# Sums over a head's features as products with a column of ones, in a one-core hybrid decoder layer

## The chip, the cores and the metric

The program runs on one core of a Trainium2 chip. The metric is the time of one execution on the device in microseconds (us); the runs of the kernel before have a median of 665.29 us.

## What is computed

One decoder layer over 256 tokens of width 1024, in float32. A normed input goes through one combined projection (`w_in`) that feeds four token mixers: A, attention; B, a chunked gated DeltaNet; C, an RWKV-7 recurrence; D, a Mamba-2 SSD. Each mixer's output goes through its own projection, is gated and summed, goes through `w_out` and is added to the input; then comes a SwiGLU feed-forward part. The change touches three sums over the 64 features of a head: RWKV's squared length of `kk` and its `bonus`, and DeltaNet's squared lengths of q and k.

```python
def l2norm(x):
    xf = x.astype(jnp.float32)
    return xf * lax.rsqrt(jnp.sum(xf * xf, axis=-1, keepdims=True) + 1e-6)
...
        o_b = gated_deltanet(l2norm(heads(g_q)) * (Dh ** -0.5), l2norm(heads(g_k)),
                             heads(g_v), beta, g_log)
...
        kk = l2norm(heads(c_k * rwkv_k_k[i]))
...
        bonus = jnp.sum(r_h * k_h * rwkv_r_k[i], axis=-1, keepdims=True) * v_h
```

## The kernel before

Every large product has a float32 weight matrix that is split in two parts, `whi` and `wlo` (rounded to a one-pass format), and a split activation. Weights come in pieces of 128x1024: SyncE loads `wraw`, ScalarE casts it to `whi`, VectorE subtracts to get `wlo`, and each piece then feeds 24 products of 256 columns on TensorE, 8 of them with `wlo`. These "large products" (`pj`, `pjt`, `pbr`, `pjo`, `pjf`; `pd` in the last stage) fill TensorE from the first to the last microsecond.

The mixers run between them. Features lie on partitions, two heads of 64 to a tile; a tile of one tensor is [128, 4, 256] (two heads by 64 features, four pairs, 256 tokens). A head's part of 64 tokens is a 64x64 block, and work on it uses 64x64 tiles of the array, two at a time. `stacked` turns such blocks over by a product with the identity, so that tokens lie on partitions: 16 calls for half of a tensor, into a PSUM tile `ptk`. Each call of a float32 product is two instructions in the trace (and two weight loads). The block is the stationary operand, the identity the moving one.

RWKV (`rwkv_mix`): `kkr` and `rkr` (tile `a`) are turned over in halves, ScalarE squares the turned `kkr` into `U`, and VectorE sums over features with TENSOR_REDUCE into `rk2` (shown as `rk`) and `bon`. Then eight groups of `pab` products make the matrix `U` that is inverted (`inverse`: a trip through DRAM as `Du`, `UL`, a loop on VectorE over `TL`, a trip as `Dz`, `TN`, and products `pq`, `pt`, `pq`, `pn`). Four chunk steps follow (`pA`, `pB`, `pH`, `pY`), then a tail of VectorE work (group norm, bonus) up to the products `py`; "c" is done behind it. DeltaNet (`gdn_mix`) has the same shape: `tokens(0)` turns `KQ[:, 0]` over, squares it (`sq`), sums it (`sse`) and keeps the turned block as `Kt`; `tokens(1)` does so for q later on, for the sum alone.

The order on each engine is not written out: a planner (class `Queue`, `Chain`, `run`) simulates the engines while the program is recorded, with a cost for each instruction in `Queue.cost`, and chooses from the ready steps of the mixers' chains and the large products. Each engine then runs its instructions in that recorded order. All are recorded in one helper, so all rows have line L180. PSUM has two banks in the pool `pa` for the mixers and two in `px`.

Of the kernel before, what the change touches and what calls it, by code (L numbers as in the profile page):

```python
# [10 lines left out]
AF = mybir.ActivationFunctionType  # L11
OP = mybir.AluOpType
AX = mybir.AxisListType
# [154 lines left out]
class Queue:  # L168
# [98 lines left out]
    def cost(self, op, a, k, n, ins, start):  # L267
        if self.idx == 0:
            w = a[1]
            t = int(start / 3.413)  # L270
            if t != self.tick:
                self.warm = t == self.tick + 1 and self.cols >= 3060
                self.tick, self.cols = t, 0.0
            one = op == "transpose" or w.dtype != F32
            self.cols += n * (1 if one else 2) * w.shape[0] / 128
            tiling = tuple(32 if x <= 32 else 64 if x <= 64 else 128 for x in (w.shape[0], math.prod(w.shape[1:])))
            if op == "transpose":
                d = 0.109 * n / 128
            elif one:
                d = 0.006 + 0.00043 * n  # L280
            elif tiling[0] == 32:
                d = 0.018
            elif tiling == (64, 64):
                d = 0.058 if n <= 64 else 0.003 + n / 1200
            else:
                d = max(0.22, 0.006 + n / 600)
            if tiling != self.tiling:

                d += 0.2 if tiling == (128, 128) else 0.14
                self.tiling = tiling  # L290
            return d * (1 if self.warm else 1.95)
        if self.idx == 1:
            if op == "tensor_tensor" or op == "tensor_sub" or op == "tensor_reduce":
                return 0.065 + 0.00105 * n if op != "tensor_reduce" else 0.07 + 0.00105 * math.prod(ins[0].shape[1:])
            if op == "scalar_tensor_tensor":
                return 0.12 + 0.00105 * n
            return 0.065 + (0.0064 if op == "reciprocal" else 0.0009) * n
        if self.idx == 2:
            d = 0.047 + 0.00088 * n + (0.1 if hasattr(k.get("scale"), "shape") or hasattr(k.get("bias"), "shape") else 0.0)
            s = _SETS.get(a[2] if len(a) > 2 else None)  # L300
            if s is not None and s != self.table:
                self.table = s
                d += 1.3
            return d
        if k.get("op") == OP.pow:
            return 0.3 + 0.165 * n
        return 0.1 + {"tensor_tensor": 0.0019, "tensor_sub": 0.00215, "tensor_copy": 0.0016}.get(op, 0.001) * n
# [3 lines left out]
def trunk(ctx: ExitStack, tc: tile.TileContext, I, out):  # L311
    nc = tc.nc
    clock = Clock(tc)
    T, V, A, G, SY = [Queue(clock, i, e) for i, e in enumerate((nc.tensor, nc.vector, nc.scalar, nc.gpsimd, nc.sync))]
# [213 lines left out]
    ones = cst.tile([128, 1], F32, name="ones")  # L528
# [61 lines left out]
    def p_(n, j=None, k=1):  # L590
        o, w = PO[n]
        if j is None:
            return PR[:, o:o + w]
        return PR[:, o + j:o + j + k]
# [35 lines left out]
    def du_rows(h):  # L630

        return bass.AP(tensor=Du.tensor, offset=Du.offset + 4160 * h, ap=[[64, 64], [8320, 16], [1, 64]])
# [8 lines left out]
    def ui(c, pp=0):  # L641

        return (c % 2) * 8 + (c // 2) * 4 + pp

    def t2(name, shape=(128, 4, 256)):
        return wk.tile(list(shape), F32, name=name, tag="t2", bufs=T2)
# [16 lines left out]
    def bank(name):  # L663
        return pa.tile([128, 512], F32, name=name, tag="pa")
# [13 lines left out]
    def halves(fn):  # L678
        for h in range(2):
            fn(h, slice(h * 64, (h + 1) * 64))  # L680
# [8 lines left out]
    def trh(out, x):  # L689

        for s in (slice(0, 64), slice(64, 128)):
            T.matmul(out[s], x[s], ident[s, s], start=True, stop=True)

    def inverse(U, N64):

        halves(lambda h, s: SY.dma_start(du_rows(h), U[s]))
        for k in range(4):
            s, o = 32 * k, 32 * (k % 2)
            G.tensor_copy(uo[s:s + 16, :, 16:32], U[s:s + 16, :, o + 16:o + 32])
        TL = wk.tile([128, 16, 16], F32, name="TL", tag="TL", bufs=1)  # L700
# [50 lines left out]
        for u in range(16):  # L751
            for h in range(2):
                T.matmul(pq[blk[2 * h + 1], u], U[blk[2 * h], u, 32:64], T16[blk[2 * h], u], start=True, stop=True)
        for h in range(2):
# [9 lines left out]
    def stacked(src, half):  # L764

        pt = bank("ptk").rearrange("p (u e) -> p u e", u=8)
        for c in (half, half + 2):
            for pp in range(4):
                trh(pt[:, ui(c, pp) - 8 * half], src[:, pp, c * 64:(c + 1) * 64])
        return pt, slice(8 * half, 8 * half + 8)  # L770

    def stacked_copy(src, dst):
        for half in range(2):
            pt, us = stacked(src, half)
            A.copy(dst[:, us], pt)
# [186 lines left out]
    def rwkv_mix():  # L962
        ck, cr, cvv = rst[0], rst[1], rst[2]
        W, Wi, a = rws["W"], rws["Wi"], rws["a"]
        kkr, ka = t2("kkr"), t2("kka")
# [25 lines left out]
        Bb, Kb, rkr = ka, Wi, kr  # L991
# [3 lines left out]
        for q in two:  # L995
            V.tensor_tensor(Kb[:, q], kr[:, q], Wi[:, q], op=OP.mult)
            yield
        for pp in range(4):
            V.scalar_tensor_tensor(rkr[:, pp], cr[:, pp], p_("rk", pp), kr[:, pp], op0=OP.mult, op1=OP.mult)
            if pp % 2:  # L1000
                yield 1
        U = t2("U", (128, 16, 64))
        rk2, bon = [wk.tile([128, 16], F32, name=n, tag=n, bufs=1) for n in ("rk2", "bon")]
        for half in range(2):
            pt, us = stacked(kkr, half)
            A.activation(U[:, us], pt, AF.Square)
            pt, us = stacked(rkr, half)
            V.tensor_reduce(bon[:, us], pt, op=OP.add, axis=AX.X)
            V.tensor_reduce(rk2[:, us], U[:, us], op=OP.add, axis=AX.X)
            yield 0  # L1010
        V.tensor_scalar(rk2, rk2, 2.0, 2e-6, op0=OP.mult, op1=OP.add)
        V.reciprocal(rk2, rk2)
        yield 0

# [1 line left out]
        for c in (0, 2, 1, 3):  # L1016
            for q in two:
# [5 lines left out]
                us = slice(ui(c, q.start), ui(c, q.stop))  # L1023
# [6 lines left out]
        wait = next(inv)  # L1030
        Vst, Bt, Kt = [t.rearrange("p q (a b) -> p (q a) b", b=64) for t in (cr, cvv, ck)]
        stacked_copy(cvv, Vst)
        yield 0
        stacked_copy(Bb, Bt)
        yield 0
        stacked_copy(Kb, Kt)
        yield wait
        yield from inv
# [4 lines left out]
        for c in range(4):  # L1043
            us = slice(ui(c), ui(c) + 4)
            cs = slice(c * 64, (c + 1) * 64)
            pA = cbank("pA")
            for pp in range(4):
                u = ui(c, pp)
# [12 lines left out]
            if c < 3:  # L1061
                pH = cbank("pH")
                for pp in range(4):
                    u = ui(c, pp)
# [10 lines left out]
            for pp in range(4):  # L1075
                u = ui(c, pp)
# [99 lines left out]
    def gdn_mix():  # L1176
# [3 lines left out]
        KQ, Vt, zs = gst_["kq"], gst_[2], gst_[3]  # L1180
        sq = t2("sq", (128, 16, 64))
        sse = wk.tile([128, 2, 16], F32, name="sse", tag="sse", bufs=1)
        store = a3("gst3", (128, 3, 16, 64))
        Kt, At, Vn = store[:, 0], store[:, 1], store[:, 2]
        DL = DLs[0]

        def tokens(kq):

            for half in range(2):
                pt, us = stacked(KQ[:, kq], half)  # L1190
                A.activation(sq[:, us], pt, AF.Square)
                if kq == 0:
                    A.copy(Kt[:, us], pt)
                yield 0
                V.tensor_reduce(sse[:, kq, us], sq[:, us], op=OP.add, axis=AX.X)
            V.tensor_scalar(sse[:, kq], sse[:, kq], 4e-6, None, op0=OP.add)

        yield KQ
        yield from tokens(0)
        yield  # L1200
        nk = wk.tile([128, 16], F32, name="nk", tag="nk", bufs=1)
        V.tensor_scalar(nk, sse[:, 0], 0.25, None, op0=OP.mult)
# [10 lines left out]
        U = t2("gU", (128, 16, 64))  # L1213
        for c2 in range(2):
            for a in range(2):
                pab = bank("pab").rearrange("p (u e) -> p u e", u=4)
                us = slice(ui(2 * a + c2), ui(2 * a + c2) + 4)
# [10 lines left out]
        for half in range(2):  # L1228
            pvn, us = stacked(Vt, half)
            V.tensor_tensor(Vn[:, us], pvn, nk[:, us, None].to_broadcast([128, 8, 64]), op=OP.mult)  # L1230
        yield 0
        yield from tokens(1)
        yield wait
        yield from inv
        yield N64
# [2 lines left out]
        for c in range(4):  # L1238
            us = slice(ui(c), ui(c) + 4)
# [538 lines left out]
    for k in "AC":  # L1778
        ytile(k)
    Chain("mix", when(has("common"), then("g", rwkv_gates())), when(lambda: len(ready_c) == 6, then("c", rwkv_mix())),  # L1780
          when(lambda: len(ready_b) == 8 and "dec" in done, then("b", gdn_mix())))
    Chain("fill", when(has("common"), scalars()), when(has("g"), attn_bias()), *[then(f"a{g}", attn[g][1]()) for g in range(2)], then("dec", decays()),
          *[then(f"d{g}", when(has("A"), mam[g][1]())) for g in range(2)])
# [14 lines left out]
    sq = cst.tile([128, 2, 4], F32, name="sq2")  # L1798
# [188 lines left out]
```

## Time and profile before

| | |
|---|---|
| median of 3 runs | 665.29 us (663.74 to 665.30) |
| profiled execution, time | 665.81 us |
| its span | 663.9 us |
| busy: PE, VectorE, ScalarE, GpSimd | 643.4, 442.9, 306.3, 44.6 us |
| mean granted TensorE clock | 0.991 |
| longest group on VectorE | `wlo`, 176 of 1.22 us: 213.8 us |
| longest group on ScalarE | `whi`, 176 of 1.05 us: 183.1 us |

PE's busy time counts modelled ends of pipelined products, so it is an upper bound. What counts is where PE waits, and what the clock was. The feed-forward part (from 475 us) and the input part (to 138 us) are the same work in the same order in both kernels.

### The profile page before, as it was taken

To read this page: it belongs to the slowest core of one execution; us is meant where nothing else is said; L and a number is where in the kernel's file an instruction comes from. 1 tells how busy PE (TensorE), PEld (TensorE's weight loads), DVE (VectorE), ACT (ScalarE), POOL (GpSimd) and SP (SyncE) were. 2 spreads that over 40 slices of the span, in tenths; PEclk is the share of its full clock that TensorE was granted. 3 is DMA by queue.
4 is the path that set the end of the run, shared out by engine and by line. 5 is a ranking of instruction groups with operands and counts; after the bars stand their busy time and mean duration, and the time that the engine had idled before them with its cause. 6 is when DMAs were issued, how large, how long until landed. Compare 5 with 4: busy or idle time off the path is not lost.

```text
span 663.9 us, 15583 instructions
## 1 busy us (share of the span) xinstructions
PE 643.4 (97%) x6677; PEld 605.7 (91%) x6677; DVE 442.9 (67%) x769; ACT 306.3 (46%) x484; POOL 44.6 (7%) x48
## 2 busy tenths in 40 slices
PE   8999999899998988999999999999999999999997
PEld 7799999899897878999999989999999999998885
DVE  4575567966864389888678367777676666664443
ACT  5465465433534254465433343444554544454331
POOL 1001003003400020100210002000000000000000
PEclk9999999989999988999999999999999999999999
DMA  8534845324182123255466433665565555555551
GB/s 287 159 128 154 281 147 160 120 65 129 41 244 69 35 64 128 96 193 160 156 168 177 136 97 97 220 223 165 158 199 189 183 189 191 190 182 181 189 178 64
DMA packets 47866, 102.80 MB, mean 155 GB/s; under 512 B 19980, under 2 KB 24501, under 8 KB 47798
## 3 DMA queue, kind: packets, MB, share of 16 engines
q1 hardware_dynamic: 47562, 101.25, 48.1%
q8 instruction: 52, 0.85, 0.5%
q10 hardware_dynamic: 236, 0.58, 0.2%
q14 instruction: 16, 0.13, 0.1%
HBM read 99.17 MB, written 4.21 MB: 156 GB/s over the span
## 4 chain that ended last, share of the span: by engine, by line
PE 85%; DVE 6%; ACT 3%; DMA 2%; issue 1%; POOL 0%; DVEq 0%; SPq 0%; ACTq 0%; POOLq 0%
PE pj L180 25%; PE pjf L180 19%; PE pd L180 9%; PE pjt L180 6%; PE pbr L180 5%; PE pjo L180 4%; PE ptk L180 2%; DVE wlo L180 2%; PE pab L180 2%; DMA TN<-Dz 1%; PE pA L180 1%; PE psx L180 1%; PE po L180 1%; PE pY L180 1%; PE pB L180 1%
## 5 line engine op out<-in xcount | busy, mean ns | idle before, releaser
L180 DVE TENSOR_TENSOR wlo<-wraw,whi 128x1024 fp32r<-128x1024 f32 x176 | 213.8, 1221 | 68.5 <-ACT whi L180 67.5
L180 ACT CAST whi<-wraw 128x1024 fp32r<-128x1024 f32 x176 | 183.1, 1049 | 143.0 <-PE pj L180 39.0
L180 PE MATMUL pj<-HT,whi 128*128 128x256 f32 x1120 | 154.3, 286 | 0.4 <-ACT HT L180 0.2
L180 PEld LDWEIGHTS pj<-HT,whi 128*128 128x128 f32 x1120 | 139.9, 189 | 5.1 <-issue 3.0
L180 PE MATMUL pjf<-HT,whi 128*128 128x256 f32 x704 | 91.2, 281 | 0.0
L180 PEld LDWEIGHTS pjf<-HT,whi 128*128 128x128 f32 x704 | 86.7, 188 | 0.1
L180 PE MATMUL pj<-HT,wlo 128*128 128x256 f32 x560 | 80.5, 284 | 0.8 <-DVE wlo L180 0.8
L180 PEld LDWEIGHTS pj<-HT,wlo 128*128 128x128 f32 x560 | 71.6, 188 | 1.6 <-DVE wlo L180 1.2
L180 PE MATMUL pd<-whi,gt 128*128 128x512 f32 x176 | 54.8, 393 | 0.0
L180 PE MATMUL pjf<-HT,wlo 128*128 128x256 f32 x352 | 49.2, 281 | 0.0
L180 PEld LDWEIGHTS pjf<-HT,wlo 128*128 128x128 f32 x352 | 44.9, 188 | 0.0
L180 PEld LDWEIGHTS pd<-whi,gt 128*128 128x128 f32 x176 | 33.0, 188 | 7.4
L180 PE MATMUL pjt<-whi,HT 128*128 128x256 f32 x256 | 37.9, 302 | 0.9 <-ACT whi L180 0.9
L180 PEld LDWEIGHTS pjt<-whi,HT 128*128 128x128 f32 x256 | 35.0, 207 | 2.2 <-ACT whi L180 1.3
L180 PE MATMUL pd<-wlo,gt 128*128 128x512 f32 x88 | 34.5, 393 | 0.0
L180 DVE TENSOR_TENSOR gu<-pjf,rB 128x512 f32<-128x512 f32 x22 | 15.2, 691 | 17.4 <-PE pjf L180 17.3
L180 PE MATMUL pjt<-wlo,HT 128*128 128x256 f32 x128 | 19.1, 286 | 2.5 <-DVE wlo L180 2.5
L180 PEld LDWEIGHTS pd<-wlo,gt 128*128 128x128 f32 x88 | 16.5, 188 | 3.8
L180 PEld LDWEIGHTS pjt<-wlo,HT 128*128 128x128 f32 x128 | 16.7, 191 | 3.0 <-DVE wlo L180 3.0
L180 ACT CAST gt<-sg 128x256 fp32r<-128x256 f32 x22 | 8.9, 406 | 20.9 <-DVE sg L180 20.9
L180 PE MATMUL pjo<-whi,ms 128*128 128x256 f32 x128 | 17.8, 284 | 0.0
L180 DVE TENSOR_TENSOR gt<-sg,gt 128x256 fp32r<-128x256 f32 x22 | 9.4, 425 | 11.8 <-ACT gt L180 11.8
(395 smaller groups left out, 836.0 us busy)
## 6 DMA issues: line engine op xcount, KB each, us to landing
wraw<-in_w_in_dram SPq DMA_DIRECT2D x86, 512.0 KB, 4.3
wraw<-in_ffn_in_dram SPq DMA_DIRECT2D x44, 512.0 KB, 3.7
wraw<-in_ffn_down_dram SPq DMA_DIRECT2D x22, 512.0 KB, 3.7
wraw<-in_w_branch_dram SPq DMA_DIRECT2D x16, 512.0 KB, 5.1
wraw<-in_w_out_dram SPq DMA_DIRECT2D x8, 512.0 KB, 4.4
D<-Dv SPq DMA_DIRECT2D x1, 1536.0 KB
E<-D SPq DMA_DIRECT2D x8, 128.0 KB, 3.4
xm<-in_x_dram SPq DMA_DIRECT2D x4, 256.0 KB, 5.2
```

The lines of the kernel that those rows point to most:

```text
L180: bi = fn(*a, **k)
```

## The change

A new function `sums` makes the sum over features with the block as the stationary operand and a column of ones as the moving one: 32 calls of one column for each tensor, into a PSUM tile `pss`. In RWKV the four `stacked` and four TENSOR_REDUCE go; ScalarE squares all of `kkr` in one instruction from SBUF (into `U`), `sums` takes `U` and `rkr`, and VectorE reads the sums from PSUM, with one more small copy for `bon`. In DeltaNet `tokens` goes; both squares and both sums come at the start, and `stacked_copy` makes `Kt` where `tokens(1)` stood. One number of the planner's cost table changes: a 64x64 call with n of at most 64 columns was 0.058 us and is 0.03 + 0.00044 n.

```diff
             elif tiling == (64, 64):
-                d = 0.058 if n <= 64 else 0.003 + n / 1200
+                d = 0.03 + 0.00044 * n if n <= 64 else 0.003 + n / 1200
...
+    def sums(*src):
+
+        ps = bank("pss")[:, :16 * len(src)].rearrange("p (k u) -> p k u", u=16)
+        for k, x in enumerate(src):
+            for c in range(4):
+                for pp in range(4):
+                    for s in (slice(0, 64), slice(64, 128)):
+                        T.matmul(ps[s, k, ui(c, pp):ui(c, pp) + 1], x[s, pp, c * 64:(c + 1) * 64], ones[s], start=True, stop=True)
+        return ps
...
+        U = t2("U", (128, 16, 64))
+        A.activation(U.rearrange("p (q a) b -> p q (a b)", q=4), kkr, AF.Square)
...
-        for half in range(2):
-            pt, us = stacked(kkr, half)
-            A.activation(U[:, us], pt, AF.Square)
-            pt, us = stacked(rkr, half)
-            V.tensor_reduce(bon[:, us], pt, op=OP.add, axis=AX.X)
-            V.tensor_reduce(rk2[:, us], U[:, us], op=OP.add, axis=AX.X)
-            yield 0
-        V.tensor_scalar(rk2, rk2, 2.0, 2e-6, op0=OP.mult, op1=OP.add)
+        ps = sums(U.rearrange("p (q a) b -> p q (a b)", q=4), rkr)
+        V.tensor_scalar(rk2, ps[:, 0], 2.0, 2e-6, op0=OP.mult, op1=OP.add)
+        V.tensor_copy(bon, ps[:, 1])
...
-        yield KQ
-        yield from tokens(0)
+
+        sqv = sq.rearrange("p (q a) b -> p q (a b)", q=4)
+        for kq in range(2):
+            yield KQ
+            A.activation(sqv, KQ[:, kq], AF.Square)
+            yield 1
+            V.tensor_scalar(sse[:, kq], sums(sqv)[:, 0], 4e-6, None, op0=OP.add)
...
-        yield from tokens(1)
+        stacked_copy(KQ[:, 0], Kt)
```

Since the planner's picture of time changes, the order of all that follows changes on every engine. Three places:

TensorE, where RWKV's sums are made (`ptk` and `pss` as above, `pab` the first group behind them; x counts calls). Before:

```order
L180 MATMUL pjt<-wlo,HT_78 128x256 x4
L180 MATMUL ptk<-ident,kkr 64x64 x16
L180 MATMUL ptk<-ident,a 64x64 x16
L180 MATMUL pjt<-wlo,HT_78 128x256 x4
L180 MATMUL pj<-HT_78,whi 128x256 x8
L180 MATMUL ptk<-ident,kkr 64x64 x16
L180 MATMUL ptk<-ident,a 64x64 x16
L180 MATMUL pab<-AR,kka 64x128 x2
```

TensorE at the same place, now:

```order
L180 MATMUL pjt<-wlo,HT_78 128x256 x4
L180 MATMUL pss<-ones,U 64x1 x32
L180 MATMUL pss<-ones,a 64x1 x32
L180 MATMUL pab<-AR,kka 64x128 x2
L180 MATMUL pab<-AR,Wi 64x128 x2
```

The twelve large products that stood between the turned blocks now come later.

ScalarE in RWKV's inverse (`kkr<-TN` and `TN<-pq` are the inverse's copies; `pn` on TensorE needs the latter). Before:

```order
L180 CAST whi<-wraw 128x1024 x2
L180 COPY kkr<-TN 32x16x32 x4
L180 CAST whi<-wraw 128x1024 x2
L180 COPY TN<-pq 32x512 x2
L180 ACTIVATE gate<-pj 128x512
```

ScalarE in RWKV's inverse, now:

```order
L180 CAST whi<-wraw 128x1024
L180 COPY kkr<-TN 32x16x32 x4
L180 COPY TN<-pq 32x512 x2
L180 ACTIVATE gate<-pj 128x512
L180 CAST whi<-wraw 128x1024
```

The two casts between the two kinds of copies have moved to behind them.

VectorE, the last rows of RWKV's tail (`kka` is RWKV's output, `bc` and `cvt` a convolution of mixer D, `xd`, `zt` also D's; `U<-py` ends the tail). Before:

```order
L180 SCALAR_TENSOR_TENSOR bc<-pj,PR,bc 128x255
L180 TENSOR_TENSOR kka<-kka,kc 128x512
L180 TENSOR_TENSOR wlo<-wraw,whi 128x1024
L180 TENSOR_TENSOR kka<-kka,grsd 128x512
L180 TENSOR_TENSOR kka<-kka,PR 128x512
L180 SCALAR_TENSOR_TENSOR bc<-pj,PR,bc 128x254
L180 TENSOR_TENSOR kka<-kka,kc 128x512
L180 SCALAR_TENSOR_TENSOR bc<-pj,PR,bc 128x253
L180 TENSOR_TENSOR wlo<-wraw,whi 128x1024 x2
L180 SCALAR_TENSOR_TENSOR bc<-pj,bc 128x256
L180 SCALAR_TENSOR_TENSOR zt<-zt,pjt 128x512
L180 SCALAR_TENSOR_TENSOR U<-py,PR,U 128x256 x4
```

VectorE, the last rows of the same tail, now:

```order
L180 TENSOR_TENSOR zt<-dx,zt 128x256
L180 SCALAR_TENSOR_TENSOR cvt<-pj,PR,cvt 128x253
L180 SCALAR_TENSOR_TENSOR bc<-pj,PR,bc 128x254
L180 TENSOR_TENSOR kka<-kka,kc 128x512
L180 TENSOR_SCALAR ms<-ms 128x1
L180 SCALAR_TENSOR_TENSOR cvt<-pj,cvt 128x256
L180 SCALAR_TENSOR_TENSOR bc<-pj,PR,bc 128x253
L180 TENSOR_TENSOR wlo<-wraw,whi 128x1024
L180 TENSOR_SCALAR zt<-zt,ms 128x256
L180 SCALAR_TENSOR_TENSOR bc<-pj,bc 128x256
L180 SCALAR_TENSOR_TENSOR U<-py,PR,U 128x256 x4
```

From the first operation behind the last `P<-pB` to `U<-py`, the tail held six `wlo` and eight `bc` operations before and holds four and four now; the rest of these have moved to behind `U<-py`.

## Rows read from the trace of the kernel before

**Rows 1.** The page, part 1 and the granted clock of part 2 (40 slices of the span, tenths).
```profile
PE 643.4 (97%) x6677; PEld 605.7 (91%) x6677; DVE 442.9 (67%) x769; ACT 306.3 (46%) x484; POOL 44.6 (7%) x48
...
PEclk9999999989999988999999999999999999999999
```

**Rows 2.** Busy time by stretch: us, PE, PEld, DVE, ACT, POOL, PEclk, DMA share, GB/s.
```profile
138.60:194.20 55.60, 54.96 (x724) 49.92 (x723) 40.24 (x82) 26.22 (x44) 13.56 (x16) 1.00 0.37 99
194.20:231.10 36.90, 34.79 (x885) 31.52 (x885) 14.90 (x28) 11.36 (x22) 1.75 (x3) 1.00 0.25 84
231.10:259.60 28.50, 23.62 (x207) 22.12 (x206) 25.50 (x51) 13.46 (x27) 3.46 (x2) 0.88 0.23 74
```

**Rows 3.** Timeline of PE: start, us, then the instructions (two for each float32 call).
```profile
138.61 1.15 PE L180 MATMUL ptk<-ident,kkr 64*64 64x64 f32 x32
...
144.20 0.44 PE L180 MATMUL pab<-AR,kka 64*64 64x128 f32 x4
...
159.31 2.08 PE L180 MATMUL ptk<-ident,kka 64*64 64x64 f32 x64
161.23 2.03 PE L180 MATMUL ptk<-ident,Wi 64*64 64x64 f32 x64
```

**Rows 4.** Single tiles: count, ns min/median/max, first and last start, array tile and shape.
```profile
L180 PEld LDWEIGHTS ptk<-ident,kkr x64: 129/135/135, 138.6 to 143.1; 64*64 64x64 f32 x64
...
L180 PEld LDWEIGHTS pst<-sc,ident x16: 132/138/138, 48.3 to 48.7; 128*64 128x64 f32 x16
...
L180 PEld LDWEIGHTS pe<-dA,C x8: 189/192/192, 166.1 to 166.9; 128*128 128x128 f32 x8
...
L180 DVE TENSOR_REDUCE sse<-sq x4: 680/686/686, 319.2 to 339.8; 128x8 f32<-128x512 f32 x4
...
L180 ACT CAST whi<-wraw x176: 1034/1049/1058, 10.6 to 651.4; 128x1024 fp32r<-128x1024 f32 x176
```

**Rows 5.** The chain that ended last, in order of time: start, us, what.
```profile
187.77 6.38 DMA TN<-Dz
194.19 1.24 PE pq L180 x79
...
251.95 5.08 PE pjt L180 x28
...
267.14 0.86 PE pyd L180 x8
...
283.83 33.61 PE pj L180 x284
```

**Rows 6.** Timeline of ACT in RWKV's inverse, and of PE behind it.
```profile
202.95 2.50 ACT L180 COPY kkr<-TN 32x512 f32<-32x512 f32 x4 [9.85 <-DVE TN L180]
205.48 1.99 ACT L180 CAST whi<-wraw 128x1024 fp32r<-128x1024 f32 x2
207.50 1.18 ACT L180 COPY TN<-pq 32x512 f32<-32x512 f32 x2
...
208.73 1.19 PE L180 MATMUL pn<-TN 32*32 32x32 f32 x62 [0.36 <-ACT TN L180]
```

**Rows 7.** Timeline of RWKV's tail: its ends on DVE, and PE's longest wait.
```profile
231.78 0.42 DVE L180 TENSOR_TENSOR P<-pB,rk 128x256 f32<-128x256 f32 x1 [2.54 <-PE pB L180]
...
251.95 0.91 PE L180 MATMUL pjt<-wlo,HT 128*128 128x256 f32 x4 [1.62 <-DVE wlo L180]
...
261.05 1.65 DVE L180 SCALAR_TENSOR_TENSOR U<-py,PR,U 128x256 f32<-128x256 f32 x4
```

**Rows 8.** Groups of DVE instructions: count, busy us, mean ns, idle before.
```profile
L180 DVE TENSOR_TENSOR wlo<-wraw,whi 128x1024 fp32r<-128x1024 f32 x176 | 213.8, 1221 | 68.5 <-ACT whi L180 67.5 <-issue 0.7
...
L180 DVE SCALAR_TENSOR_TENSOR bc<-pj,PR,bc 128x254 f32<-128x254 f32 x4 | 1.9, 470 | 0.0
```

**Rows 9.** Busy time by stretch around the first fall of the clock (columns as in rows 2).
```profile
129.00:132.40 3.40, 1.75 (x11) 1.41 (x10) 3.40 (x10) 1.09 (x3) 0.00 (x0) 1.00 0.45 154
132.40:135.80 3.40, 3.39 (x18) 3.39 (x18) 3.40 (x7) 0.00 (x0) 0.00 (x0) 0.57 0.51 163
```

**Rows 10.** Timeline: DeltaNet's output, from its last products to its first use.
```profile
417.49 2.08 PE L180 MATMUL py<-ident,O 64*64 64x64 f32 x64
...
421.42 1.28 DVE L180 TENSOR_TENSOR yB<-gvz,yB 128x512 fp32r<-128x512 f32 x2
...
436.18 1.12 PE L180 MATMUL pbr<-yB,whi 128*128 128x256 f32 x8
```

More of the change, by code (lines that the diff above doesn't have):

```diff
@@ L1001, in rwkv_mix @@
                 yield 1
-        U = t2("U", (128, 16, 64))
         rk2, bon = [wk.tile([128, 16], F32, name=n, tag=n, bufs=1) for n in ("rk2", "bon")]
-        for half in range(2):
-            pt, us = stacked(kkr, half)
-            A.activation(U[:, us], pt, AF.Square)
-            pt, us = stacked(rkr, half)
-            V.tensor_reduce(bon[:, us], pt, op=OP.add, axis=AX.X)
-            V.tensor_reduce(rk2[:, us], U[:, us], op=OP.add, axis=AX.X)
-            yield 0
-        V.tensor_scalar(rk2, rk2, 2.0, 2e-6, op0=OP.mult, op1=OP.add)
+        ps = sums(U.rearrange("p (q a) b -> p q (a b)", q=4), rkr)
+        V.tensor_scalar(rk2, ps[:, 0], 2.0, 2e-6, op0=OP.mult, op1=OP.add)
+        V.tensor_copy(bon, ps[:, 1])
         V.reciprocal(rk2, rk2)
@@ L1185, in gdn_mix @@
         DL = DLs[0]
[L1187 to L1196, printed above, removed]
-        yield KQ
-        yield from tokens(0)
+        sqv = sq.rearrange("p (q a) b -> p q (a b)", q=4)
[4 more added lines that the diff above has]
+            V.tensor_scalar(sse[:, kq], sums(sqv)[:, 0], 4e-6, None, op0=OP.add)
         yield
```

## The prediction

> **What bounds the kernel now.** I read the page first: PE is busy for 97% of the span, VectorE for 67%, and the granted clock dips in three slices of 40 [rows 1]. So the time is PE's own work plus the places where PE waits or runs at the lower clock, and an engine that is relieved counts only where PE waits for it. Next I cut the span into stretches. From RWKV's sums to the first `pq`, PE is busy for 54.96 of 55.60 us; through the inverse and the four chunk steps for 34.79 of 36.90 us; through RWKV's tail for 23.62 of 28.50 us, at a mean clock of 0.88 [rows 2]. At full clock the tail holds 23.62 x 0.88 = 20.8 us of PE work, so 7.7 us are lost there, the largest loss of the kernel. VectorE is the reason: the tail lasts from the last `P<-pB` to `U<-py`, 231.78 to 261.05 us, 29.3 us, and PE's longest wait in it, 1.62 us, is for a `wlo` [rows 7]. The other two losses are on a chain: `pq` starts at 194.19, when the DMA `TN<-Dz` lands, with no gap between them [rows 5], and `pn` waits for ScalarE's copy `TN<-pq`, which stands behind two casts of 1.99 us [rows 6]. The eight reductions that the change removes are not in any of these places. What the change does to the time is therefore PE's own sum, and what the new order does at these three places.
>
> **PE's own work.** A turned block costs, from the starts of two neighbouring runs of 32 calls, (161.23 - 159.31) / 32 = 0.060 us per call [rows 3]. RWKV's four `stacked` (64 calls) and DeltaNet's four in `tokens` (64) go: 128 x 0.060 = 7.7 us. `stacked_copy` for `Kt` brings 32 back: +1.9 us. The 128 calls of one column are new. No row shows a 64x64 tile with one column, so I bound it. Above: the same tile with 64 columns, 0.060. Below: the 32x32 tile, where 64 calls of `pq` take 1.24 us [rows 5], 0.019 each. The nearest row is `pst`, 64 columns of weights and 8 moving: 16 instructions start between 48.3 and 48.7 us [rows 4], 0.4/15 = 27 ns each, 0.053 for a call of two. And its weight load takes 138 ns, that of a turned block 135, that of a 128-column block 192: the load goes by the columns of the weights, and the change leaves those at 64. So I take 0.057, close to the upper end: 128 x 0.057 = 7.3 us. PE's work changes by -7.7 + 1.9 + 7.3 = **+1.5 us**, with ends of -3.4 (at 0.019) and +1.9 (at 0.060).
>
> The Trainium skill speaks against this part of the change. "TensorEngine Tiling (Array Packing)", Instruction Overhead, says that a matmul with one column takes as long as one with 60; by it the sums would cost what the turned blocks cost and the work would be +1.9. The row of `pst` agrees so far as it goes (8 columns, hardly cheaper than 64).
>
> **What leaves the other engines.** Eight reductions of 0.68 us [rows 4] leave VectorE and one small copy comes: about -5 us, but at 140 to 145 and 319 to 340 us, where PE does not wait for VectorE. Cover: PE has large products queued there, so this is worth nothing by itself. ScalarE squares a whole tensor at once, about 1.05 us (its cast of the same 1024 elements, [rows 4]). In DeltaNet this square now stands ahead of PE's `pss`, with large products queued in front; without them PE would wait up to 1.05 us, twice. DVE's reading of `pss` waits for PE, and behind it stand the reciprocal and the first `U<-pab`; these wait for `pab` anyway. `pss` holds one of two PSUM banks until two reads of about 0.2 us are over, while the first `pab` fills the other: nothing.
>
> **RWKV's chain up to `pq`.** The order puts twelve large products and four turns of `cvt` behind the `pab` groups that stood among them. A large product is 33.61/284 = 0.118 us [rows 5]. The last `pab` is done 12 x 0.118 + 0.4 + 0.2 (sums) = 2.0 us sooner. On VectorE two operations of `bc` now stand inside the inverse's loop, 2 x 0.47 [rows 8], so `TN` lands about 1.1 us sooner, at 193.1. PE, in turn, has 24 large products fewer ahead of `pq` (2.8 us) and 0.2 less for the sums: it arrives 3.0 us sooner, at 191.2. So a wait of **+1.9 us** that is not there before (0 if the chain keeps pace, 3.0 if the landing does not move). Behind the waiting `pq` stand only large products, and nobody needs those sooner.
>
> **The inverse.** The two casts between the copies are gone from ScalarE's order, so `pn` can come 2 us sooner after `pq` [rows 6]; PE has eight large products fewer in between (0.95 us). Net **-1.0 us** of loss (0 to -2).
>
> **The tail.** VectorE's list for it loses two `wlo` (2 x 1.22) and four `bc` (4 x 0.47) [rows 8]; of the rest, one `xd` and two short `yD` go and one `lm`, one `dx` and a one-column operation come, about -0.3. Together 4.6 us off 29.3. PE's list gains sixteen large products (1.9) and one more group `pyd` (0.86, [rows 5]): 23.5 us. The stretch of 28.5 us would be 23.9 by VectorE and 23.5 by PE; two engines so nearly level wait for each other (VectorE itself is idle for 3.0 of 28.5 us now), so I take 26.0. The loss falls from 7.7 to 2.5: **-5.2 us** (0 to -7.2). The displaced operations go to 260 to 317 us, where PE has large products without a break.
>
> DeltaNet's chain starts later against the large products, and its output is due with 76 of them ahead instead of 140. From the start of `py` to `yB` takes 422.70 - 417.49 = 5.2 us [rows 10]; 1.9 (`py`) + 76 x 0.118 = 10.9 us now cover it, so no wait.
>
> **Sum:** +1.5 + 1.9 - 1.0 - 5.2 = -2.8 us. The profiled execution took 665.81 us, 0.5 above the median of 665.29; I set the difference against the median: **662.5 us**.
>
> **Rivals.**
> *The tail stays* (0.18). One mechanism: the tail is bound by VectorE, and if it still takes 29.3 us there, since the chain to it or the short waits between the tail's steps fill the freed time, the 5.2 us do not come. For: VectorE is already idle for 3 us within it. Against: nearly all of its rows stand back to back. Price: 662.5 + 5.2 = 667.7, slower. It decides once the tail on VectorE is over 28 us.
> *The clock falls at the sums* (0.22). In the 3.4 us before the first fall PE was busy for 1.75 us; then it ran at a mean of 0.57 of full speed for 3.4 us, part of that at the 1.2 GHz level [rows 9]: 0.43 x 3.4 = 1.5 us lost. In the sums PE is occupied with weight loads but streams one column each, for 3.6 us in RWKV and twice 1.8 us in DeltaNet; before, it streamed 64. No row shows what the clock makes of such a stretch. One fall gives 664.0, two 665.5: no measurable change.
> *One column is cheap* (0.12). If a call costs 0.019 to 0.030 as on the smaller tile, the work is -3.4 to -2.0 instead of +1.5: 657.6 to 659.0, faster. Against it stands the weight load of 64 columns.
> *Nothing but the sums* (0.10). Waits move and cancel, PE's own work remains: 665.3 + 1.5 = 666.8. It is also what comes out if the new order does nothing at these places.
>
> **How the numbers follow.** The forecast case has 0.38 and spans 660.5 to 664.5. About 0.3%, 2.0 us here, is what a measurement of this kernel can tell from no change. Faster (below 663.3): 0.30 of the forecast, all of the cheap column and 0.02 of the clock: 0.44. Within: 0.08 of the forecast, 0.17 of the clock, 0.08 of the last case and 0.02 of the tail: 0.35. Slower: the rest, 0.21. The range reaches from the cheap column at 0.020 (658.0) to just over the staying tail (668.0); it leaves out less than 2 in 10.
>
> **What would show it.** Starts of `pss` 57 ns per call apart, or 20 to 30; `pq` with a wait of about 2 us for `TN<-Dz` near 193 us; ScalarE's two kinds of inverse copies without casts between them; from the last `P<-pB` to `U<-py` 25 to 27 us instead of 29.3; no wait at `pbr<-yB`. The prediction is wrong if the lower clock appears right behind the sums, if the tail is still near 29 us, or if a new wait of several us stands in DeltaNet's inverse.

## The result: slower, by two falls of the clock

The changed kernel takes 672.4 us in the median of nine runs (668.4 to 674.2), the kernel before 665.3 us in nine runs beside it. The ratio is 1.0083 with a 95% interval of 1.0059 to 1.0108: slower by 0.83%, which is 5.5 us (the two medians by themselves are 7.1 us apart), where the forecast was 662.5 us and the range ended at 668.0. The profiled execution took 670.89 us with a span of 669.0.

The page of the changed kernel, part 1 and the granted clock by slices of the span:

```profile
PE 647.8 (97%) x6741; PEld 611.2 (91%) x6741; DVE 437.7 (65%) x762; ACT 306.2 (46%) x481; POOL 43.0 (6%) x48
...
PEclk9999999989999999999699999999999999999999
```

VectorE has lost 5.2 us of work as forecast (442.9 before, [rows 1]), and PE has 4.4 us more. The row of the clock has changed its shape: the dips of slices 15 and 16, RWKV's tail, no longer show (one of the two falls there is left, at 248.2 to 251.6 us), and a deeper one stands in slice 20, where DeltaNet makes its sums.

Cut into the stretches of [rows 2] and the rest up to the first `pjo` (columns as there):

```profile
138.39:194.95 56.56, 53.52 (x700) 48.41 (x699) 35.71 (x78) 23.09 (x41) 11.64 (x16) 0.97 0.36 90
194.95:231.94 36.99, 34.54 (x892) 31.06 (x893) 15.60 (x25) 11.36 (x20) 0.62 (x1) 1.00 0.30 95
231.94:259.09 27.15, 24.96 (x252) 24.04 (x254) 23.41 (x47) 11.66 (x23) 4.63 (x4) 0.94 0.22 62
259.09:453.00 193.91, 190.50 (x2350) 184.93 (x2345) 139.70 (x249) 87.30 (x126) 14.07 (x14) 0.97 0.50 155
...
138.39:142.14 3.75, 3.75 (x129) 3.75 (x130) 0.00 (x0) 1.55 (x4) 0.00 (x0) 1.00 0.02 4
142.41:145.82 3.41, 3.41 (x33) 3.08 (x30) 1.35 (x7) 0.00 (x0) 0.00 (x0) 0.50 0.00 0
...
324.07:327.58 3.51, 3.51 (x64) 3.49 (x64) 0.00 (x0) 0.88 (x1) 0.00 (x0) 0.50 0.07 30
327.58:333.55 5.97, 5.97 (x30) 5.97 (x29) 2.78 (x5) 1.64 (x2) 2.92 (x1) 0.50 0.39 114
```

The fifth row is RWKV's sums: PE is busy for 3.75 of 3.75 us at full clock. The sixth is what follows 0.3 us later: 3.41 us at 0.50, the 1.2 GHz level, with PE still busy all the time. The last two rows are DeltaNet's second sums and the large products behind them: 9.5 us at 1.2 GHz, again without a gap. The whole of that fall is 323.3 to 333.6 us. What it does to single steps stands in PE's timeline:

```profile
138.39 2.03 PE L180 MATMUL pss<-ones,U 64*64 64x1 f32 x64
140.28 2.01 PE L180 MATMUL pss<-ones,a 64*64 64x1 f32 x64
142.14 0.43 PE L180 MATMUL pab<-AR,kka 64*64 64x128 f32 x4
...
143.64 0.64 PE L180 MATMUL pab<-AR,kka 64*64 64x128 f32 x4
144.07 0.64 PE L180 MATMUL pab<-AR,Wi 64*64 64x128 f32 x4
...
147.22 0.39 PE L180 MATMUL pab<-AR,kka 64*64 64x128 f32 x4
147.44 0.39 PE L180 MATMUL pab<-AR,Wi 64*64 64x128 f32 x4
...
168.51 0.55 PE L180 MATMUL pty<-ident,MT 128*128 128x128 f32 x3 [0.81 <-DVE MT L180]
...
180.34 1.12 PE L180 MATMUL pl<-lm,C 128*128 128x512 f32 x2 [1.55 <-POOL lm L180]
...
194.95 1.29 PE L180 MATMUL pq<-TN,uo 32*32 32x32 f32 x128 [0.47 <-DMA TN<-Dz]
...
199.88 1.21 PE L180 MATMUL pj<-HT,whi 128*128 128x256 f32 x8 [1.09 <-issue]
...
203.34 0.26 PE L180 MATMUL pt<-TN 32*32 32x32 f32 x8 [1.09 <-issue]
...
320.83 2.03 PE L180 MATMUL pss<-ones,sq 64*64 64x1 f32 x64
322.79 0.80 PE L180 MATMUL pj<-HT,whi 128*128 128x256 f32 x4
324.07 3.58 PE L180 MATMUL pss<-ones,sq 64*64 64x1 f32 x64 [0.48 <-ACT sq L180]
327.58 1.22 PE L180 MATMUL pj<-HT,whi 128*128 128x256 f32 x4
...
334.61 2.05 PE L180 MATMUL pj<-HT,whi 128*128 128x256 f32 x16
...
441.64 1.12 PE L180 MATMUL pbr<-yB,whi 128*128 128x256 f32 x8
```

From start to start a group of `pab` takes 0.43 us inside the fall and 0.22 behind it. Eight groups, from 142.14 to 145.49 (3.35 us), would have taken 1.75: with a little at the `pjt` behind them, 1.7 us are lost. In DeltaNet the second sums take 3.51 us (324.07 to 327.58) where the first took 1.96, 1.55 lost; from 327.58 to 334.61 there are 36 large products, worth 36 x 0.118 = 4.25 of the 7.03 us, 2.8 lost: 4.3 together. Two falls cost about 6.0 us by these rows, about as much as the kernel lost. The rest of the report is the test of that reading.

### The profile page after: what moved, and what is told of

Its sections match the earlier page's. It is cut to its first block, busy times and chain, and to the rows that moved or that the text cites. A ratio compares the mean times of both kernels' runs of the same rounds, so it can differ in the third digit from the quotient of the medians.

```text
span 669.0 us, 15699 instructions
## 1 busy us (share of the span) xinstructions
PE 647.8 (97%) x6741; PEld 611.2 (91%) x6741; DVE 437.7 (65%) x762; ACT 306.2 (46%) x481; POOL 43.0 (6%) x48
## 4 chain that ended last, share of the span: by engine, by line
PE 83%; DVE 8%; ACT 2%; issue 2%; DMA 1%; POOL 1%; SPq 0%; DVEq 0%; ACTq 0%; POOLq 0%
PE pj L180 24%; PE pjf L180 19%; PE pd L180 9%; PE pjt L180 7%; PE pbr L180 6%; PE pjo L180 3%; PE pab L180 2%; DVE wlo L180 2%; PE ptk L180 2%; PE pss L180 1%; DVE TL L180 1%; PE psx L180 1%; PE pq L180 1%; PE pY L180 1%; PE pA L180 1%
## 5 line engine op out<-in xcount | busy, mean ns | idle before, releaser
L180 PE MATMUL pj<-HT,wlo 128*128 128x256 f32 x560 | 82.0, 287 | 3.3 <-DVE wlo L180 3.3
L180 PE MATMUL pjt<-whi,HT 128*128 128x256 f32 x256 | 36.4, 294 | 0.7 <-ACT whi L180 0.7
```

The costliest lines, as they stand in the source:

```text
L180: bi = fn(*a, **k)
```

## The experiments

**64 columns of ones.** The sums keep their weights, their number and their place; only the moving operand is 64 columns wide, taken from a block of ones that the program holds anyway. The four groups of blocks (`c`) are taken in the sequence 0, 2, 1, 3, so that the columns are written upwards. A call then writes 64 columns of the sums' PSUM tile, of which the next calls overwrite all but the first. The planner is told the old number, so that the order on every engine is that of the changed kernel, row for row.

```diff
+            if op == "matmul" and str(self.name(a[0])).startswith("pss"):
+                n = 1
...
+        w = 64 if wide else 1
...
-            for c in range(4):
+            for c in (0, 2, 1, 3):
                 for pp in range(4):
+                    j = 16 * k + ui(c, pp)
                     for s in (slice(0, 64), slice(64, 128)):
-                        T.matmul(ps[s, k, ui(c, pp):ui(c, pp) + 1], x[s, pp, c * 64:(c + 1) * 64], ones[s], start=True, stop=True)
+                        T.matmul(full[s, j:j + w], x[s, pp, c * 64:(c + 1) * 64], c_("onesbd")[s, s] if wide else ones[s], start=True, stop=True)
```

> The changed kernel with the same order on every engine; only the moving operand of all sums is 64 columns of ones instead of one (the block of ones of a constant). Each call then writes 64 columns, of which the next calls overwrite all but the first, so that the sums are the same. Theory: the clock falls because the sums stream one column per weight load. Then both falls go: the granted clock is 1.00 in the 7 us behind RWKV's sums and in the 13 us from DeltaNet's sums; the second half of DeltaNet's sums takes 2.0 us, not 3.6; a call costs 0.060 instead of 0.059. Eight groups of pab at 0.43 instead of 0.22 us each cost 1.7 us, and DeltaNet's 9.5 us from the second sums on are worth 5.2 us at full clock, 4.2 us lost: 5.9 us together, so 672.4 - 5.9 = 666.5 us. By the sum of the prediction, which had no fall at the sums, it should be 662.9. Rival (order, waits or the weight loads themselves are the cause): the falls stay and the time stays at 672.

Measured: 664.84 us, ratio to the kernel before 0.9994 (0.9968 to 1.0020). Against the changed kernel's 1.0083 that is 0.89% of 665.3 = 5.9 us (uncertain by about 2.4), the size expected from the falls. Stretches of this run (columns as above), from the fall that stands ahead of the sums to behind DeltaNet's:

```profile
132.47:142.71 10.24, 9.62 (x56) 8.87 (x58) 6.46 (x15) 2.99 (x6) 0.00 (x0) 0.50 0.34 102
142.71:149.25 6.54, 6.54 (x164) 6.24 (x162) 2.66 (x8) 0.00 (x0) 0.00 (x0) 1.00 0.01 3
322.20:333.88 11.68, 11.14 (x186) 10.66 (x185) 3.91 (x9) 4.59 (x5) 2.92 (x1) 1.00 0.47 171
```

PE's timeline of this run:

```profile
141.55 2.59 PE L180 MATMUL pss<-C,U 64*64 64x64 f32 x64
...
145.84 0.38 PE L180 MATMUL pab<-AR,kka 64*64 64x128 f32 x4
146.07 0.38 PE L180 MATMUL pab<-AR,Wi 64*64 64x128 f32 x4
...
196.97 1.29 PE L180 MATMUL pq<-TN,uo 32*32 32x32 f32 x128 [0.61 <-DMA TN<-Dz]
...
322.20 2.08 PE L180 MATMUL pss<-C,sq 64*64 64x64 f32 x64
324.21 0.75 PE L180 MATMUL pj<-HT,whi 128*128 128x256 f32 x4
325.50 2.08 PE L180 MATMUL pss<-C,sq 64*64 64x64 f32 x64 [0.54 <-ACT sq L180]
```

The clock is 1.00 behind both sums, `pab` is at its 0.22 us a group, and DeltaNet's second sums take 2.01 us, with the wait of 0.54 us for ScalarE still there. Weights, number of calls, the order of the instructions and the wait for the second square are those of the changed kernel; what differs is the number of columns that PE streams (and writes), and the sequence of the blocks. The one-column sums that are left in the next two runs have that sequence too and keep their falls. So the one-column calls make the falls, and not the order, that wait or the weight loads. (In this profiled execution the fall that stands ahead of the sums in both kernels, [rows 9], lasted 10.2 us instead of 3.4 and reached into the first sums; it took 668.1 us, and ten of the other eleven runs were faster, by up to 5.8 us.)

**64 columns in RWKV only, or in DeltaNet only.** Same order again. The edit of the second, against the run above; the first has `wide=False` in DeltaNet's line instead.

```diff
-        ps = sums(U.rearrange("p (q a) b -> p q (a b)", q=4), rkr)
+        ps = sums(U.rearrange("p (q a) b -> p q (a b)", q=4), rkr, wide=False)
```

> As the run with 64 columns of ones everywhere, but only in RWKV; DeltaNet's sums keep one column. Order as in the changed kernel. Theory: the fall behind RWKV's sums goes (1.7 us), the one from DeltaNet's sums on stays with its 10 us at the lower clock: 670.7 us. Rival (the fall in RWKV costs nothing, since what follows waits for the DMA of the inverse anyway): 672.4.

> 64 columns of ones in DeltaNet only; RWKV's sums keep one column. Order as in the changed kernel. Theory: the 10 us at the lower clock in DeltaNet go (4.2 us), RWKV's fall stays: 668.2 us. PE still waits 0.5 us for ScalarE's second square. Rival (the fall there comes from that wait for ScalarE together with the second sums): the lower clock stays, 672.

Measured: 668.20 us, ratio 1.0044 (1.0017 to 1.0071), with RWKV's sums wide; 666.73 us, 1.0009 (0.9984 to 1.0034), with DeltaNet's. RWKV's fall is worth 0.39% (2.6 us) with DeltaNet's still there and 0.15% (1.0 us) without it, DeltaNet's 0.74% and 0.50% (4.9 and 3.3 us). Each ratio is uncertain by about 0.26%, so a difference of two by about 0.36%: DeltaNet's part is clear of that, and RWKV's is not in both ways of taking it; both go with the 1.7 and 4.3 us of the rows. In DeltaNet the clock stays up although PE still waits 0.54 us for the second square, which rules out that wait as the cause.

**One narrow sum.** All wide but the first of DeltaNet's two.

```diff
-            V.tensor_scalar(sse[:, kq], sums(sqv)[:, 0], 4e-6, None, op0=OP.add)
+            V.tensor_scalar(sse[:, kq], sums(sqv, wide=kq == 1)[:, 0], 4e-6, None, op0=OP.add)
```

> As the run with 64 columns of ones everywhere, in the same order on every engine, but the first of DeltaNet's two sums (k, 32 calls, 1.9 us) has one column; q's sum and RWKV's keep 64. It asks with nothing else changed whether 1.9 us of one-column calls between large products make the clock fall, which the run with DeltaNet's sums apart showed under another order. Theory A (a short stretch is enough): a fall of 3.4 us behind k's sum, about 1.7 us, ratio to the kernel before 1.002. Theory B (it takes the longer stretch): no fall between 320 and 335 us, ratio 0.999 as with 64 columns everywhere.

Measured: 667.27 us, ratio 1.0028 (0.9999 to 1.0057), which is theory A's number; but the profiled execution, with a span of 661.3 us, shows theory B. The sum starts at 317.2 us in it, and the stretch behind reads:

```profile
318.70:336.00 17.30, 16.74 (x232) 15.70 (x230) 9.08 (x23) 5.63 (x6) 3.26 (x2) 1.00 0.28 92
```

One trace and the times do not agree, so both seem to happen. Of its twelve runs four have a mean granted clock of 0.996 to 0.997 and take 662.5 to 664.6 us, eight have 0.984 to 0.992 and take 667.1 to 671.9; of the twelve with all sums wide only three are at 0.992 or below. Which of the eight lost it at this very sum the runs do not tell. But the traces of the other runs show that a stretch of 1.9 us can be enough: in the changed kernel itself the fall begins at 323.3 us, 0.5 us behind the first of DeltaNet's two sums and before the second has started. So such a stretch is followed by a fall in some traces and not in this one.

**DeltaNet's sums apart.** The sum of q goes back to where its turned blocks stood, some 22 us behind that of k, both with one column; the planner's number is 0.058 again.

```diff
...
-        for kq in range(2):
-            yield KQ
+        def tokens(kq):
             A.activation(sqv, KQ[:, kq], AF.Square)
             yield 1
             V.tensor_scalar(sse[:, kq], sums(sqv)[:, 0], 4e-6, None, op0=OP.add)
+        yield KQ
+        yield from tokens(0)
...
         stacked_copy(KQ[:, 0], Kt)
+        yield 0
+        yield from tokens(1)
```

> The changed kernel, one column of ones, DeltaNet's sum of q moved back to where the turned q stood before (behind the pab groups and the turned blocks of K), so that DeltaNet's sums are two stretches of 1.9 us with other products for some 15 us between; number of the planner 0.058 us. RWKV's 3.7 us of sums stay as they are. Theory: a stretch of 1.9 us between large products is too short for a fall, so DeltaNet's 10 us at the lower clock go and RWKV's fall stays: ratio as with 64 columns in DeltaNet only, 1.001 (1.000 to 1.004). Rival: each of the two stretches makes a fall of its own of 3.4 us or more, ratio 1.006 to 1.010.

Measured: 673.33 us, ratio 1.0135 (1.0087 to 1.0182). Stretches of this run: k's sums, what follows, q's sums, what follows.

```profile
320.20:322.62 2.42, 2.42 (x69) 2.40 (x69) 0.34 (x2) 0.11 (x1) 0.00 (x0) 1.00 0.56 222
322.62:326.03 3.41, 3.41 (x19) 3.41 (x18) 2.18 (x3) 1.04 (x1) 1.15 (x1) 0.50 0.37 126
343.80:346.51 2.71, 2.68 (x71) 2.54 (x70) 0.48 (x2) 1.52 (x3) 0.00 (x0) 1.00 0.30 113
346.51:349.93 3.42, 3.42 (x19) 3.42 (x18) 0.83 (x1) 0.67 (x1) 0.00 (x0) 0.50 0.44 117
```

The rival was right: each stretch of 1.9 us has a fall of its own, of 3.4 us. Two short ones replace the long one. The time is above the expected 1.006 to 1.010 as well, since the new order brings another wait, 3.05 us of "issue" ahead of `pt` in DeltaNet's inverse, with a fall behind it.

**The planner's number back.** One line: a 64x64 call is 0.058 us again instead of 0.030, the sums stay narrow.

> The changed kernel with the planner's number for a 64x64 call put back to 0.058 us, close to the 0.059 that a call takes; the sums are as in the changed kernel, with one column, but the planner orders anew from the first pab on. Theory (the sums themselves make the clock fall): both falls stay, 17 us of the stretch at the lower level, and the time is 672 within the 3 us that another order can make. Rival (the price of 0.030, half of what a call takes, made the planner put too little work on PE around the sums, and the order is the loss): the falls or the waits at pq and pj go, 666.

Measured: 673.24 us, ratio 1.0114 (1.0077 to 1.0151). Both falls are there (141.4 to 144.8 and 322.3 to 332.6 us), and PE now waits 2.0 us at DeltaNet's `pq` with a fall behind it. Putting the price right did not win the loss back.

**Large products between the sums.** The sums are cut every four calls, the planner may step in there, and its number is 0.058.

```diff
...
                         T.matmul(ps[s, k, ui(c, pp):ui(c, pp) + 1], x[s, pp, c * 64:(c + 1) * 64], ones[s], start=True, stop=True)
+                    if pp % 2:
+                        yield 0
...
```

> The changed kernel with one column of ones as it is, but the sums are cut into pieces of 4 calls with a place between them where the planner may put other work, and its number for a 64x64 call is 0.058 us. It puts 24 large products between RWKV's 64 calls of U and a, and 32 between DeltaNet's 64 of sq; the order behind that changes too. Theory (the clock falls because nothing but one-column calls runs for 3.7 us): with large products between them both falls behind the sums go, and the time is that of 64 columns of ones within what another order makes, ratio to the kernel before 0.999 +- 0.004 (663 to 668 us). Rival (a one-column call lowers the clock whatever runs beside it, by the total of such calls): both falls stay, ratio 1.008.

Measured: 679.38 us, ratio 1.0213 (1.0182 to 1.0244), far from both. The stretch of RWKV's sums and what follows, then the fall among DeltaNet's sums (from 321.50 us to this fall the clock is 1.00):

```profile
137.35:145.04 7.69, 7.69 (x159) 7.39 (x160) 2.45 (x2) 2.61 (x5) 0.00 (x0) 1.00 0.44 139
145.04:160.00 14.96, 14.96 (x241) 13.73 (x241) 12.46 (x32) 5.59 (x13) 2.45 (x3) 1.00 0.13 39
...
328.95:335.78 6.83, 6.83 (x50) 6.57 (x49) 1.38 (x3) 1.39 (x2) 3.10 (x1) 0.50 0.39 124
```

In RWKV, with 28 large products among 64 calls, the fall is gone. In DeltaNet, with 32 among 64, it has shrunk from 10.2 to 6.8 us. So for the falls the theory held half-way. The time went elsewhere: the order behind RWKV's sums is new, the tail takes 35.3 us (236.18 to 271.52), and PE waits 5.24 us for `zt`, 1.85 for `yD` and 2.8 by "issue" (for nothing that the profile shows), with further falls. A time from a kernel whose whole order moved says little about one cause in it.

**Three versions meant to beat both kernels.** The first tells the planner the 64 columns. The second (two runs: planner told 64 columns, planner told one) turns k over and reduces it as before, because the turned block is needed as `Kt` anyway, and sums only q by products. The third changes RWKV alone, wide, and leaves DeltaNet as it was.

```diff
...
+        A.activation(sqv, KQ[:, 1], AF.Square)
+        yield 1
+        V.tensor_scalar(sse[:, 1], sums(sqv)[:, 0], 4e-6, None, op0=OP.add)
+        for half in range(2):
+            pt, us = stacked(KQ[:, 0], half)
+            A.activation(sq[:, us], pt, AF.Square)
+            A.copy(Kt[:, us], pt)
+            yield 0
+            V.tensor_reduce(sse[:, 0, us], sq[:, us], op=OP.add, axis=AX.X)
...
```

> 64 columns of ones in all sums, and the planner is told so: it counts 64 columns and 0.058 us for each call and orders the rest anew (with one column at 0.030 us kept for nothing). Theory: no falls behind the sums, as in the run with the old order: ratio 0.999; the honest price is worth at most the short waits around pq, 0.5 us. Rival: the order made with the price of 0.030 costs several us on its own, which the falls hid: 0.994.

> A version that should beat both: 64 columns of ones; DeltaNet's k is turned over, squared and summed by VectorE as in the kernel before, since its turned block is needed anyway as Kt, and only q is summed by products. That leaves PE with as many calls of 64x64 as before (64 in RWKV, 64 in DeltaNet), 32 fewer than in the changed kernel: 32 x 0.060 = 1.9 us less. VectorE gets two reductions of 0.68 us back, where PE does not wait for it. Theory: no falls behind the sums, 1.9 us below the run with 64 columns everywhere: ratio 0.996 to 0.997 (662.5 to 663.5 us). Rival (PE's own work is not what the time follows here): 0.999, as with 64 columns.

> As the version with k turned over and reduced and q summed by products of 64 columns, but with the planner's count of one column at 0.030 us, so that the order up to DeltaNet is that of the run with 64 columns everywhere (the version before had another tail, 31.7 us instead of 27.2, and ended at 1.005). Theory (that tail was the loss): the tail is 27 us again, and with 32 calls fewer than the changed kernel the ratio is 0.996. Rival (DeltaNet's new order is the loss): 1.003 or above.

> The change in RWKV alone, with 64 columns of ones; DeltaNet turns over, squares and reduces as in the kernel before. On every engine the order up to DeltaNet is that of the run with 64 columns everywhere, so the tail of RWKV has the new order too. PE then has as many 64x64 calls as the kernel before, 32 fewer than the changed kernel. Theory (the time follows PE's own work where PE does not wait): 32 x 0.060 = 1.9 us below the run with 64 columns everywhere, ratio 0.996 (663 us), with no fall behind the sums and U<-py some 27 us behind the last P<-pB. Rival (the order of DeltaNet, made anew, decides): 0.999 or above.

Measured: 1.0028 (1.0007 to 1.0050) for the new plan with 64 columns; 1.0051 (1.0024 to 1.0078) and 1.0005 (0.9984 to 1.0026) for the lean one; 1.0008 (0.9981 to 1.0035) for RWKV alone. None is faster than the kernel before. The tail did differ between the two lean runs, by 5.5 us in the traces: with the planner told 64 columns RWKV's tail goes from 229.41 to 261.09 us, with PE waiting 3.37 us for `lm`; told one, from 229.24 to 255.41. But 32 calls fewer did not give their 1.9 us: lean_keep waits 3.55 us ("issue") at DeltaNet's `pt`, and RWKV alone 2.12 us for `TN<-Dz` at DeltaNet's `pq`. The waits speak for the rival of those runs, DeltaNet's new order; no run takes them away alone, so that is argued and not shown.

## Why the prediction was wrong

**The step that failed** is the clock's term in the sum, which the prediction put at nothing. It saw the risk, described the place and gave it a chance of 0.22, but the sum of +1.5 + 1.9 - 1.0 - 5.2 runs at full clock behind the sums, and no row was given for that. The runs show 5.9 us there: that is what the changed kernel loses against the same order with 64 columns, 1.0083 against 0.9994. As a rival it was priced too low as well: a fall at 1.5 us and two at 3.0, from one fall of 3.4 us [rows 9]. RWKV's cost 1.7, close to that. DeltaNet's lasted three times as long, and cost 4.3. Priced so, this case would have ended at 662.5 + 6.0 = 668.5, slower, and not within 0.3%. "No row shows what the clock makes of such a stretch" was true, and then the price needed an upper end: a fall that lasts longer than the one seen. The other terms, taken below one by one, were off together by less: -2.8 us was forecast for them, and the run with 64 columns stands at -0.4.

The Trainium skill points elsewhere: "TensorE: Matmul & The Clock Gate", HAM oscillation — how this bites in real kernels, looks for the loss in gaps in which PE is idle. RWKV's sums had none, 3.75 of 3.75 us busy and a fall behind them. The measurement decides here.

**A one-column call costs nearly what a 64-column call costs.** 138.39 to 142.14 us for 64 calls are 0.059 us each: taken 0.057, between the bounds, and the case of a cheap column (0.019 to 0.030) is out. The weights were of 64 columns in both. In DeltaNet 32 calls take 1.96 us with one column (320.83 to 322.79) and 2.01 with 64 (322.20 to 324.21, the wide run). The rule of the Trainium skill that the prediction weighed ("TensorEngine Tiling (Array Packing)", Instruction Overhead) says the same as these rows. PE's own work is 128 x 0.059 - 7.7 + 1.9 = +1.8 us instead of +1.5.

**The wait ahead of `pq`** (+1.9). PE has lost 56.56 - 53.52 = 3.04 us by idling in that stretch, 0.64 before [rows 2]: +2.4. The size was right by luck, for it stands at other places: `TN` did not land sooner but at 194.95, where PE waits 0.47 us for it, and PE did not arrive at 191 but stopped on the way, 0.81 us for `MT` and 1.55 us for GpSimd's `lm`. `MT` comes 3.1 us later than before and `lm` 3.9 us later. Most of that stands in PE's own steps ahead of them. `po`, which `MT` is made from, starts 28.4 us behind the start of the sums, 25.6 before; in the run with only RWKV's sums wide it is 26.8, so 1.6 us of it are RWKV's fall and the rest is the new order. The second `pd` ahead of `lm` starts at 175.76 us, 172.27 before. VectorE delays `MT` and the start of the inverse's loop as well. First `MT` in the trace of before, then the changed kernel:

```profile
165.05 0.29 DVE L180 TENSOR_TENSOR MT<-po,sm 128x128 f32<-128x128 f32 x1 [5.08 <-PE po L180]
```

```profile
167.18 0.69 DVE L180 TENSOR_TENSOR xd<-mx,sc 128x512 f32<-128x512 f32 x1 [1.42 <-ACT mx L180]
...
168.18 0.28 DVE L180 TENSOR_TENSOR MT<-po,sm 128x128 f32<-128x128 f32 x1
...
171.52 0.17 DVE L180 TENSOR_SCALAR ems<-ems 128x8 f32<-128x8 f32 x1 [1.09 <-ACT ems L180]
...
172.00 0.17 DVE L180 TENSOR_SCALAR TL<-UL 128x15 f32<-128x15 f32 x1
```

The new order has put `xd` and a `bc` right ahead of `MT` and another `bc` right ahead of the loop, and VectorE stops there for ScalarE. The loop begins at 172.00, 169.54 before; the `ems` that stands ahead of it comes from PE's `pe`, 4.1 us later than before (170.32 instead of 166.26). The prediction counted two `bc` inside the loop and did not look at what stands ahead of it. With all sums wide `pq` starts 55.4 us behind the start of the sums instead of 56.6.

**The inverse** (-1.0). ScalarE's two kinds of copies, with columns as in [rows 6]:

```profile
204.39 2.50 ACT L180 COPY kkr<-TN 32x512 f32<-32x512 f32 x4 [10.24 <-DVE TN L180]
207.34 1.18 ACT L180 COPY TN<-pq 32x512 f32<-32x512 f32 x2 [0.45 <-PE pq L180]
```

The casts between them are gone as the order said, and `pn` does not wait for the copy any more. The 0.97 us that PE waited for it before are saved. But in the stretch PE idles for 2.45 us where it idled for 2.12 (the first row below): two waits of 1.09 us by "issue" stand there, at `pj` and `pt`, where one of 1.05 us stood before. The gain was taken by the next thing that was late. The stretches of the kernel before up to the last `P<-pB`, from there to `U<-py`, and from there to the first `pjo` (columns as in [rows 2]):

```profile
194.19:231.78 37.59, 35.47 (x900) 32.14 (x901) 14.92 (x29) 11.66 (x22) 1.75 (x3) 1.00 0.25 83
231.78:261.05 29.27, 24.39 (x238) 22.93 (x240) 26.95 (x53) 13.75 (x26) 3.46 (x2) 0.88 0.25 80
261.05:447.60 186.55, 183.92 (x2269) 177.83 (x2265) 137.71 (x244) 83.63 (x121) 13.75 (x14) 1.00 0.50 157
```

**The tail** (-5.2). Its ends on VectorE:

```profile
231.94 0.42 DVE L180 TENSOR_TENSOR P<-pB,rk 128x256 f32<-128x256 f32 x1 [0.51 <-PE pB L180]
...
259.09 1.81 DVE L180 SCALAR_TENSOR_TENSOR U<-py,PR,U 128x256 f32<-128x256 f32 x4 [0.17 <-PE py L180]
```

27.15 us instead of 29.3 [rows 7], just above "25 to 27". PE idles for 27.15 - 24.96 = 2.2 us in it, 4.9 before, and one fall of the clock (16 products of `pjt` in 3.20 us, 1.3 lost) is left of two (1.3 and 1.4 lost): -2.7 and -1.4, together -4.1. This was the one term that brought something, and it was the rival "the tail stays" that was wrong. One reading in it was not right: PE's longest wait in the tail before was not the 1.62 us for `wlo` [rows 7] but 2.37 us for `zt`, also on VectorE. Now it waits there 1.22 us for `lm` and 0.97 us for a `wlo`. And the operations that left the tail were not free: the prediction put them at 260 to 317 us, where PE should not wait, but PE waits there 1.50 us for a `wlo`. That wait belongs to the next paragraph's sum. The wait for `zt` before, and the one for `wlo` now:

```profile
244.89 0.44 PE L180 MATMUL pty<-ident,zt 128*128 128x128 f32 x2 [2.37 <-DVE zt L180]
```

```profile
266.57 1.21 PE L180 MATMUL pj<-HT,wlo 128*128 128x256 f32 x8 [1.50 <-DVE wlo L180]
```

**DeltaNet's output** is not waited for: `pbr<-yB` starts at 441.64 without a gap, as forecast. The square cost a wait of 0.48 us once, with only four large products ahead of it; bound 1.05 twice. From 259.09 us to the first `pjo` PE idles 3.41 us where it was 2.6 before: +0.8.

**The sum.** +1.8 (work) + 2.4 + 0.3 - 4.1 + 0.8 = +1.2 us without the falls behind the sums, where -2.8 was forecast; with the falls +7.2. Measured are 314.61 - 309.00 = 5.6 us from the sums to the first `pjo`; the 1.6 us between I could not assign. The idle terms together (+2.4 + 0.3 - 2.7 + 0.8) agree with the two profile pages (span less PE's busy time is 20.5 us before, 21.2 now), so the excess is in what I put down to PE's work and the clock. The runs with 64 columns test the +1.2: ratio 0.9994, between -2.1 and +1.3 us. So the forecast of -2.8 is outside what was measured even with the falls away. Most of what the shorter tail gave went into PE's own work and into waits on the way to `pq`, and the "nothing but the sums" case was nearer.

## What to carry to other kernels

Replacing a product that streams 64 columns by one that streams a single column saved TensorE next to nothing here, with the weights as they were (0.059 instead of 0.060 us), and it cost the clock of what followed. If a sum must go through the array, try as many columns as are free: here 64 columns of ones, 63 of them overwritten, took the whole loss away. And where a planner makes the order, compare only kernels whose order is the same: the two lean runs, which hold the same instructions in two orders, are 0.46% apart, half of what the falls cost.

## What was not expected of the hardware

- The clock fell with PE busy throughout: 3.75 of 3.75 us ahead of RWKV's fall. The wide sums, with the same calls at the same places and no fall behind them, show that what was streamed decided it, not a gap. The other traces bear it out: in the four with RWKV's one-column sums in one piece (the changed kernel, DeltaNet alone wide, the sums apart, the price back) a fall begins within 0.6 us behind them, and in none of the seven with 64 columns there does one begin within 40 us.
- At the 1.2 GHz level the sums themselves slowed down nearly as much as the groups of `pab`, though they stream one column: 3.51 instead of 1.96 us for 32 calls. Their weight loads take up to 228 ns there, against 135 in RWKV's sums at full clock.
- The scatter between executions of one kernel is mostly the clock. Over the 57 runs of the five kernels that have the changed kernel's order, time rises by 0.92 us for each microsecond of full clock lost (665 us times one minus the mean granted clock), with a correlation of 0.94; from 662.3 us at a mean clock of 0.998 to 674.2 at 0.981. The kernel before has mean clocks of 0.981 to 0.995 over the 80 runs taken beside the experiments. A difference of 0.3% between two kernels can be one fall, more or less, in the median execution.
- A fall has no fixed length: 3.4, 6.8 and 10.2 us appear, also at the same place of the same kernel's order (DeltaNet's sums: 10.2 us in the changed kernel, 6.8 with only RWKV's wide). What sets the length these runs do not tell.
